# Overlapping the four token mixers of a hybrid diffusion block, with fillers that load up to four weight tiles ahead

## The chip, the cores and the metric

The kernel runs on one core of one Trainium2 chip. The metric is the device time of one execution in microseconds (us), from the core's own clock; less is better. Each kernel was timed in several executions, and one further execution was taken with the hardware profiler.

## The reference

The block has two layers. Each normalises the tokens (512 latent, 256 context, 1024 channels), projects them with one wide matrix `w_in`, runs four token mixers side by side on slices of that projection, merges them, and ends with a feed-forward part of 4096 channels:

```python
for l in range(DEPTH):                       # 2 layers
    hl = rmsnorm(x, ln1_g[l]) * (1 + sc1) + sh1          # sc, sh, g from c @ w_mod
    hc = rmsnorm(xc, ln1_g[l]) * (1 + csc1) + csh1
    zl, zc = hl @ w_in[l], hc @ w_in[l]
    ya = hyena(zl[..., :1536])               # long convolution by FFT, 2 orders
    yb = global_attention(...)               # 4 heads, 2 key heads, latent sees latent + context
    yc = mlstm(...)                          # 4 heads, both directions
    yd = window_attention(...)               # 8 heads, 2 key heads, band of 128
    acc = sum(sigmoid(gate[n]) * (y[n] @ w_up[l, n]) for n in range(4))
    x = x + g1 * (acc @ w_out[l])
    x = x + g2 * (relu(h2 @ w1 + b1) ** 2 @ w2 + b2)     # h2: normed, modulated x
return rmsnorm(x, final_g)
```

Context tokens go through the same weights, in the first layer to the end and in the second only as far as latent tokens read them.

## The kernel before, in words

All arithmetic is in 32-bit. A weight tile of 128 x 512 numbers (256 KB) is loaded by one DMA into a raw tile (four buffers), a high part is cast from it on ScalarE (ACT, L193), and the low rest is formed on GpSimd (POOL, L177); the pair sits in one of six buffers (`wp`, L112; `load`, L309). A projection (`proj`, L323) multiplies such a pair with the high and the low part of the tokens: 12 matmuls of 512 columns per half weight block, 24 where the 256 context columns come along.

The kernel is written as Python generators that a planner plays out in order of a clock of its own (`clk`). Each generator emits some instructions and yields the time after which its next step may go (the constants in `WT`, L38). The planner's order is what TensorE (PE) executes: every matmul is tied behind the one emitted before it (`in_order`, L202). The other engines' orders are made by the framework's scheduler from the same program.

There are two kinds of work. The **main line** is the mixers, one after the other: window attention (`wa`), global attention (`ga`), mLSTM (`ml`), Hyena (`hy`). `run` (L1551) plays one generator to its end. Wherever its next step isn't due, `fill_step` (L1528) plays one step of a **filler**: the queue `jobs` holds gate projections (`gt`) and the merges `mg3`, `mg1`, `mg2` of mixers that are done, `mods` holds the projection that gives the modulation (`mod`), `side` the spectrum of Hyena's filters (`spec`). Fillers must have their weights loaded ahead: `prefetch` (L1492) walks the queue and keeps at most two of each kind loaded or running, and a filler counts as ready `WT["lw"]` = 7.0 after its load was issued.

A mixer takes its own weights through `intake` (L709): it issues the two loads of its first column block, yields `LEAD` = 7.0, and then, block by block, issues the loads of the next block ahead of the projection of the present one. A flag (`busy`) lets only one intake run at a time. `wa` and `ga` go by four groups of query heads; in `wa` a group is 12 steps of scores, softmax and values (8 in the second layer), and in `ga` 6 (4). Each group but the last has in its middle the intake of the next group's query (`next_query`, `rows`). `pipe` (L1467) keeps two of a group's generators alive at once. `ml` goes by four heads, `mix(h)` beside `head(h + 1)`, whose intake takes three blocks; `hy` by four channel tiles, each two convolutions with tables that it loads at its very start (`hyena_branch`, L1303; the loads are L1318).

At the layer's level (L1955 to L1982) a loop makes one mixer's generator, runs it to its end, then appends the merge units of that mixer to `jobs`. After `wa` it first plays fillers until `side` is empty. Behind the last mixer `drain` plays what is left of the fillers, and the last merge, the output projection and the feed-forward part follow. Pools that two mixers share: 17 tiles of 768 columns (`slot`), 8 of 1024 (`big`), and in PSUM two double-bank tiles (`p2`), from which projections, scores and transposed scores all come.

Of the kernel before, what the change touches and what calls it, by code (L numbers as in the profile page):

```python
# [25 lines left out]
SEQ = 512  # L26
CTX = 256
# [4 lines left out]
HY0, GA0, ML0, WA0, GT0 = 0, 1536, 2560, 4624, 5392  # L32
LAT = (0, SEQ)
CTXS = (SEQ, CTX)
NT, NS = 17, 8
LEAD = 7.0
PACE = {"hy0": 6, "hy1": 2.55, "mlp": 7}
WT = {"wa1": 4.0, "wa2": 1.4, "waq": 6.0, "wak": 3.0, "gap": 3.19, "gaq": 2.0, "ga1": 4.0, "ga2": 1.4, "gas": 6.0,  # L38
# [4 lines left out]
class Unit:  # L43


    def __init__(self, lab, body, pre=None, kind=None, end=False, after=0.0):
        self.lab, self.body, self.pre, self.kind, self.end, self.after = lab, body, pre, kind, end, after
        self.loaded = False

# [54 lines left out]
def hybrid_block(ctx: ExitStack, tc: tile.TileContext, I, C, out, dbg=None, stop=None):  # L106
# [10 lines left out]
    cnt, ph, clk, last, busy = [0], ["pre"], [0.0], [None], [False]  # L117
# [32 lines left out]
    def acc_tile(segs, filler=False):  # L150

        if filler:
            return [(t0, n, pf1()[:, :n]) for t0, n in segs]
        w, t = span(segs), p2()
        return [(w.start, w.stop - w.start, t[:, w])]
# [189 lines left out]
    def span(segs):  # L345
        a = min(s[0] for s in segs)
        b = max(s[0] + s[1] for s in segs)
        return slice(a, b)
# [357 lines left out]
    def hview(hH, hL):  # L706
        return lambda k: (hH[:, k, :], hL[:, k, :])

    def intake(l, specs, mov, paired=None):  # L709

        def weights(col, segs, permute, use):
            w = I["w_in"][l][:, col : col + P]
            return [load((lambda raw, x=x: permute(raw, x)) if permute else wcols(w, x)) for x in range(2)]

        while busy[0]:
            yield 0.4
        busy[0] = True
        ahead = weights(*specs[0])
        if paired:
            second = weights(*specs[1])  # L720
        yield LEAD
        for i, (col, segs, permute, use) in enumerate(specs):
            W = ahead
            if paired and i < 2:
                if i == 0:
                    Ws = W, second
                    ps2 = [acc_tile(t[1]) for t in specs[:2]]
                    yield from paired(ps2, Ws, mov)
                else:
                    ahead = weights(*specs[2])  # L730
                use(ps2[i])
                continue
            if i + 1 < len(specs):
                ahead = weights(*specs[i + 1])
            ps = acc_tile(segs)
            yield from proj(ps, W, mov)
            use(ps)
        busy[0] = False
# [33 lines left out]
    def window_branch(l, vt, mov, segs, ymk, late, paired):  # L772
        w = span(segs)
# [79 lines left out]
        def next_query(j):  # L853
            yield from intake(l, [query(j)], mov)
            yield WT["waq"]
            Q[j] = stack_q(rope2(*Q[j], segs), segs)
# [56 lines left out]
        for j in range(4):  # L913
            items = [step(j, i, r) for i in range(nblk) for r in range(2)]
            if j < 3:
                items.insert(3, next_query(j + 1))
            yield from pipe(items)

    def global_branch(l, vt, mov, segs, ymk):
        w = span(segs)  # L920
# [111 lines left out]
        for h in range(4):  # L1032
            items = [step(h, i) for i in range(nblk)]
            if h < 3:
                items.insert(2, rows(1 if h == 1 else None, h + 1))
            yield from pipe(items)

    def mlstm_branch(l, vt, mov, segs, ymk):

        w = span(segs)  # L1040
# [8 lines left out]
        for x in range(2):  # L1049
            H, L = (t.rearrange("p k n -> p (k n)") for t in whalf())  # L1050
            nc.gpsimd.memset(H.bitcast(F32), 0.0)
            nc.gpsimd.memset(L.bitcast(F32), 0.0)
            quad = lambda t: t.rearrange("p (k g c) -> p k g c", k=4, g=4)
            low(quad(H)[:, :, :, 0:4], quad(L)[:, :, :, 0:4], quad(raw[:, x * 64 : x * 64 + 64]), heng=nc.vector)
            W.append([t.rearrange("p (k n) -> p k n", k=4) for t in (H, L)])
        pg = acc_tile(full)
        yield from proj(pg, W, mov)
        gb = tiny(8, "gb")
# [239 lines left out]
        yield from pipe([columns(), head(0)])  # L1298
        yield WT["mlh"]
        for h in range(4):  # L1300
            yield from pipe([mix(h)] + ([head(h + 1)] if h < 3 else []))

    def hyena_branch(l, vt, mov, segs, ymk, near_end):  # L1303
        tabs = {}
        for n in (SEQ, CTX) if CTXS in segs else (SEQ,):
            kt, nb = n // 256, n // P
            fw = [big(name="dft") for _ in range(2)] if n == SEQ else None
            t = big(name="dft") if n == CTX else None
            tv = []
            for j, nm in enumerate(("ap", "am", "tp", "tm")):  # L1310
                k = kt if j < 2 else nb
                c = n if j < 2 else n // 2
                if n == SEQ:
                    b_ = big(name="dft") if j >= 2 else fw[j]
                    v = b_.rearrange("p (k n) -> p k n", k=k)
                else:
                    v = t[:, j * 256 : (j + 1) * 256].rearrange("p (k n) -> p k n", k=k)
                nc.sync.dma_start(v, C[f"{nm}{n}"].rearrange("(k p) n -> p k n", p=P))  # L1318
                tv.append(v)
            tabs[n] = tv  # L1320
        w = span(segs)
        U = {}

# [87 lines left out]
                yield WT["hy5"]  # L1411
                U[ct].append(None)

        yield from inputs(0)
        yield WT["hy5"]
        if len(segs) > 1:
            for ct in range(4):
# [71 lines left out]
    jobs, side, mods = deque(), deque(), deque()  # L1489
    cur = [None, 0.0, None]  # L1490

    def prefetch():  # L1492

        for q, kind in ((jobs, "w"), (mods, "r")):
            n = 1 if cur[0] is not None and cur[0].kind == kind else 0
            for u in itertools.islice(q, 6):
                if u.pre is None:
                    continue
                if n >= 2 or not u.loaded and u.after > clk[0] + 1e-6:
                    break  # L1500
                if not u.loaded:
                    ph[0] = u.lab
                    u.pre()
                    u.loaded, u.after = True, clk[0] + WT["lw" if kind == "w" else "lr"]
                n += 1
# [6 lines left out]
    def next_fill():  # L1512

        if cur[0] is not None:
            return cur[1]
        return min([q[0].after for q in queues()] + [1e9])
# [11 lines left out]
    def fill_step():  # L1528
# [19 lines left out]
        ph[0] = mine  # L1548
        return True

    def run(lab, gen, pace=0):  # L1551

        ready, i = clk[0], 0
        while True:
            if ready <= clk[0] + 1e-6:
                if WT["eager"] and cur[0] is None and cur[2] is None and side and side[0].after <= clk[0]:
                    fill_step()
                ph[0] = lab
                try:
                    ready = next(gen) + clk[0]  # L1560
                except StopIteration:
                    return
                i += 1
                if pace and i % pace == 0:
                    fill_step()
            elif not fill_step():
                clk[0] = min(ready, max(next_fill(), clk[0] + 0.05))
# [37 lines left out]
    def merge_units(l, n, mov, segs, yd, gd=None, first=False):  # L1605
# [38 lines left out]
        for m in range(KD):  # L1644
            if gd is None:
                us += gate_units(l, n, m, mov, segs, tanh_to(m), after)
            us.append(Unit(f"mg{n}x{l}", body(m), pre(m), "w", end=True, after=after))
        return us

    def last_merge(l, n, gd, segs, yd, out_):  # L1650
# [262 lines left out]
    for l in range(DEPTH):  # L1913
# [38 lines left out]

        if l == 0:
            first_jobs()
        yds = {}  # L1955
        for n, lab, branch in ((3, "wa", window_branch), (1, "ga", global_branch), (2, "ml", mlstm_branch),
                               (0, "hy", hyena_branch)):
            yds[n], mk = ymaker(l, n, segs)
            res, extra = [], []
            if n == 3:  # L1960
                extra = [late, by_pieces(full, hdone) if l else by_halves]
            elif n == 0:
                merge = last_merge(l, 0, gd[0], segs, yds[0], res)
                extra = [lambda: next(merge)]
            strand = branch(l, vt, mov, segs, mk, *extra)
            if l and n == 3:
                strand = pipe(before + [then(hdone, full, first_jobs), strand], 9)
            run(f"{lab}{l}", strand, pace=PACE.get(f"{lab}{l}", 0))
            if n == 3 and l == 0:
                vturn(False)  # L1970
            if n == 2 and l == 0:
                vloads(True, nc.sync)
                vloads(False, nc.sync)
            if n == 0 and l == 0:
                vturn1(True)
                vturn1(False)
            while n == 3 and side:
                if not fill_step():
                    clk[0] = max(next_fill(), clk[0] + 0.05)
            if n:  # L1980
                jobs.extend(merge_units(l, n, mov, segs, yds[n], gd.get(n), first=n == 3))
        drain()  # L1982
        sc2 = mod_scale(l, vt, 4, "ln2_g")
        run(f"mg0x{l}", merge)
        ts(modT[l][:, 16:24, :], modT[l][:, 16:24, :], 0.5, None, ALU.mult)
        ph[0] = f"out{l}"
        if l + 1 < DEPTH:
            mods.extend(mod_units(l + 1, range(4)))
        hH = hp.tile([P, KD, TOT], F32R, tag="hH", name=uid("hH"))
# [80 lines left out]
```

## Time and profile before

| | before |
|---|---|
| median of three runs | 3309.09 us (3302.64 to 3313.1) |
| the profiled execution, its own time | 3312.71 us |
| its span, first to last instruction | 3310.9 us |
| PE busy | 3101.9 us, 94% of the span |
| weight loads into PE | 2624.0 us, 79% |
| VectorE (DVE), ACT, POOL busy | 1388.3, 1130.3, 1371.1 us |
[...]

A row of the stage view gives, for a stretch of the span, its length, each engine's busy time with the number of instructions in it, then the granted TensorE clock in parts of full speed, the busy share of the 16 DMA engines and their GB/s. A row of a timeline gives start, duration, engine, line, operation, out<-in and the count; in brackets stands how long the engine sat idle before it and what ended that.

The stages of the first layer's mixers are, by the first and last matmul of each: `wa` to 414 us, `ga` 425 to 693, `ml` 693 to 979, `hy` 983 to 1239. In the second layer they are `wa` to 2222, `ga` 2225 to 2424, `ml` 2424 to 2667, `hy` 2672 to 2843.

### The profile page before, as it was taken

To read this page: it belongs to the slowest core of one execution; us is meant where nothing else is said; L and a number is where in the kernel's file an instruction comes from. 1 tells how busy PE (TensorE), PEld (TensorE's weight loads), DVE (VectorE), ACT (ScalarE), POOL (GpSimd) and SP (SyncE) were. 2 spreads that over 40 slices of the span, in tenths; PEclk is the share of its full clock that TensorE was granted. 3 is DMA by queue.
4 is the path that set the end of the run, shared out by engine and by line. 5 is a ranking of instruction groups with operands and counts; after the bars stand their busy time and mean duration, and the time that the engine had idled before them with its cause. 6 is when DMAs were issued, how large, how long until landed. Compare 5 with 4: busy or idle time off the path is not lost. (4 is left out here: it accounts for less than half of the span.)

```text
span 3310.9 us, 48561 instructions
## 1 busy us (share of the span) xinstructions
PE 3101.9 (94%) x18320; PEld 2624.0 (79%) x18320; DVE 1388.3 (42%) x2920; ACT 1130.3 (34%) x2132; POOL 1371.1 (41%) x1126
## 2 busy tenths in 40 slices
PE   7888989899999999999999987899999999989999
PEld 5777778788888888788888876777777788778887
DVE  6644522554444454411222266434454434442223
ACT  5434423234332122322222254333343422243333
POOL 4422332324354453444433355223333455555553
PEclk9999999999999999899999988999999999989999
DMA  7343443333243455222222334444333343823332
GB/s 269 106 116 98 123 149 92 94 103 104 77 146 91 146 176 184 65 73 74 71 76 74 92 103 116 143 138 114 99 108 100 108 136 116 266 74 96 99 96 80
DMA packets 556922, 380.24 MB, mean 115 GB/s; under 512 B 45177, under 2 KB 503870, under 8 KB 556688
## 3 DMA queue, kind: packets, MB, share of 16 engines
q1 hardware_dynamic: 556056, 376.98, 37.9%
q8 instruction: 145, 2.38, 0.3%
q14 instruction: 89, 0.73, 0.1%
q10 hardware_dynamic: 632, 0.16, 0.0%
HBM read 307.52 MB, written 63.75 MB: 112 GB/s over the span
## 5 line engine op out<-in xcount | busy, mean ns | idle before, releaser
L177 POOL TENSOR_TENSOR mlp__wL<-mlp__raw,mlp__wH 128x512 fp32r<-128x512 f32 x268 | 354.6, 1324 | 469.3 <-ACT mlp__wH L193 321.8
L193 ACT CAST mlp__wH<-mlp__raw 128x512 fp32r<-128x512 f32 x268 | 166.1, 621 | 514.9 <-PE mlp__p L215 365.4
L177 POOL TENSOR_TENSOR gt__wL<-gt__raw,gt__wH 128x512 fp32r<-128x512 f32 x128 | 168.1, 1319 | 278.7 <-ACT gt__wH L193 220.2
L215 PE MATMUL mlp__p<-out__hL,mlp__wH 128*128 128x512 f32 (+1 forms) x784 | 272.3, 358 | 9.6 <-DVE out__hL L517 8.5
L215 PE MATMUL mlp__p<-out__hH,mlp__wH 128*128 128x512 f32 (+1 forms) x784 | 271.5, 358 | 1.8 <-ACT out__hH L516 1.8
L180 DVE SCALAR_TENSOR_TENSOR mlp__x<-mlp__p,modT,mlp__x 128x512 f32<-128x512 f32 (+1 forms) x169 | 106.3, 656 | 323.8 <-PE mlp__p L215 323.8
L215 PE MATMUL mlp__p<-mlp__y,mlp__wH 128*128 128x512 f32 (+1 forms) x672 | 232.0, 356 | 0.0
L215 PE MATMUL mlp__p<-mlp__aL,mlp__wH 128*128 128x512 f32 (+1 forms) x672 | 231.2, 355 | 0.0
L177 DVE TENSOR_TENSOR mlp__aL<-mlp__mq,mlp__y 128x768 fp32r<-128x768 f32 (+1 forms) x64 | 82.7, 1292 | 335.1 <-ACT mlp__y L193 335.0
L215 PE MATMUL mlp__p<-out__hH,mlp__wL 128*128 128x512 f32 (+1 forms) x784 | 181.8, 355 | 0.0
L215 PE MATMUL gt__m<-mod__hH,gt__wH 128*128 128x512 f32 (+1 forms) x512 | 172.8, 353 | 8.1 <-DVE spec__filt L177 3.2
L215 PEld LDWEIGHTS mlp__p<-out__hL,mlp__wH 128*128 128x128 f32 x784 | 151.4, 193 | 35.2 <-DVE out__hL L517 12.5
L215 PEld LDWEIGHTS mlp__p<-out__hH,mlp__wH 128*128 128x128 f32 x784 | 151.5, 193 | 23.9 <-issue 2.2
L215 PE MATMUL gt__m<-mod__hL,gt__wH 128*128 128x512 f32 (+1 forms) x512 | 167.6, 343 | 0.0
L177 POOL TENSOR_TENSOR ml__wL<-ml__raw,ml__wH 128x512 fp32r<-128x512 f32 x64 | 84.5, 1321 | 190.6 <-ACT ml__wH L193 171.0
L215 PE MATMUL mlp__p<-mlp__y,mlp__wL 128*128 128x512 f32 (+1 forms) x672 | 155.8, 354 | 0.0
L215 PEld LDWEIGHTS mlp__p<-out__hH,mlp__wL 128*128 128x128 f32 x784 | 135.3, 193 | 19.7
L215 PEld LDWEIGHTS mlp__p<-mlp__y,mlp__wH 128*128 128x128 f32 x672 | 126.8, 189 | 20.1 <-issue 2.4
L215 PEld LDWEIGHTS mlp__p<-mlp__aL,mlp__wH 128*128 128x128 f32 x672 | 127.1, 189 | 18.0
L193 ACT CAST gt__wH<-gt__raw 128x512 fp32r<-128x512 f32 x128 | 79.3, 619 | 178.2 <-DMA gt__raw<-in_w_in_dram 113.0
L215 PEld LDWEIGHTS mlp__p<-mlp__y,mlp__wL 128*128 128x128 f32 x672 | 115.0, 189 | 17.6
L215 PEld LDWEIGHTS gt__m<-mod__hH,gt__wH 128*128 128x128 f32 x512 | 98.7, 193 | 21.6 <-DVE spec__filt L177 5.2
(567 smaller groups left out, 7906.4 us busy)
## 6 DMA issues: line engine op xcount, KB each, us to landing
mlp__raw<-in_mlp_w_dram SPq DMA_DIRECT2D x240, 256.0 KB
mod__raw<-in_w_mod_dram SPq DMA_DIRECT2D x160, 256.0 KB
gt__raw<-in_w_in_dram SPq DMA_DIRECT2D x128, 256.0 KB
ml__raw<-in_w_in_dram SPq DMA_DIRECT2D x64, 256.0 KB
hy__raw<-in_w_in_dram SPq DMA_DIRECT2D x48, 256.0 KB
spec<-spec__kk SPq DMA_DIRECT2D x80, 128.0 KB
ga__raw<-in_w_in_dram SPq DMA_DIRECT2D x32, 256.0 KB
hy__spec<-spec SPq DMA_DIRECT2D x16, 512.0 KB
```

The source lines that it names most:

```text
L177: (eng or nc.vector).tensor_tensor(o, a, b, op)
L180: nc.vector.scalar_tensor_tensor(o, a, s, b, op0, op1)
L193: nc.scalar.copy(H, src)
L215: in_order(nc.tensor.matmul(ps, lhsT=a, rhs=b, start=start, stop=stop_), cost)
```

## The change

The four mixers of a layer become generators of one `pipe` of depth four under a single `run`. Each is wrapped in `staged`, which polls until a hint names it: `wa` at once, `ga` from an item put at place 3 of `wa`'s last group, `ml` from place 2 of `ga`'s last group, `hy` from beside `mix(3)` of `ml`. What stood behind a mixer in the loop (appending its merges, waiting for `side`, some small loads) now stands at its generator's end. `intake` sets the fillers' depth to two when it begins and to four when it has issued its last block's loads, and calls `prefetch` there, ahead of that block's projection. Merges with a stored gate (`mg2`) stay at two. `ml` yields `LEAD` between loading its gate weights and projecting them, and `hy` loads its tables once `ml` has ended, instead of first thing.

```diff
+    def hint(n):
+        near.add(n)
+        yield 0.0
 def intake(l, specs, mov, paired=None):
-        busy[0] = True
+        busy[0], room[0] = True, 2
...
             if i + 1 < len(specs):
                 ahead = weights(*specs[i + 1])
+            else:
+                room[0], mine = 4, ph[0]
+                prefetch()
+                ph[0] = mine
...
 # window_branch, last group          (NEAR = 3)
+            else:
+                items.insert(NEAR, hint("ga"))
 # global_branch, last group
+            else:
+                items.insert(2, hint("ml"))
 # mlstm_branch
+        yield LEAD
         pg = acc_tile(full)
...
-            yield from pipe([mix(h)] + ([head(h + 1)] if h < 3 else []))
+            yield from pipe([mix(h)] + ([head(h + 1)] if h < 3 else [hint("hy")]))
 # hyena_branch
-        for n in (SEQ, CTX) if CTXS in segs else (SEQ,):
+        def tables(n):
...
+        def late_tables():
+            while "ml" not in ended:
+                yield 0.3
+            for n in (SEQ, CTX) if CTXS in segs else (SEQ,):
+                tables(n)
-        yield from inputs(0)
+        yield from pipe([inputs(0), late_tables()])
 # prefetch
-                if n >= 2 or not u.loaded and u.after > clk[0] + 1e-6:
+                if n >= (room[0] if kind == "w" and not u.wide else 2) or not u.loaded and u.after > clk[0] + 1e-6:
                     break
+    def staged(lab, n, strand, first=None):
+        while n not in near:
+            yield 0.3
+        if first:
+            first()
+        while True:
+            ph[0] = lab
+            try:
+                lat = next(strand)
+            except StopIteration:
+                break
+            if begun_[-1:] != [lab]:
+                begun_.append(lab)
+            yield lat
 # the layer's loop
+        def mixer(n, lab, branch):
...
+            yield from staged(f"{lab}{l}", lab, strand, (lambda: vturn(False)) if n == 1 and l == 0 else None)
+            while n == 3 and side:
+                yield 0.2
...
             if n:
-                jobs.extend(merge_units(l, n, mov, segs, yds[n], gd.get(n), first=n == 3))
+                jobs.extend(merge_units(l, n, mov, segs, yd, gd.get(n), first=n == 3))
+            ended.add(lab)
+        run("", pipe([mixer(*a) for a in ((3, "wa", window_branch), (1, "ga", global_branch), (2, "ml", mlstm_branch),
+                                          (0, "hy", hyena_branch))], 4), pace=lambda: PACE.get(begun_[-1], 0))
         drain()
```

## Rows read from the trace of the kernel before

**Rows 1.** The page: span and engines' busy time.

```profile
span 3310.9 us, 48561 instructions
PE 3101.9 (94%) x18320; PEld 2624.0 (79%) x18320; DVE 1388.3 (42%) x2920; ACT 1130.3 (34%) x2132; POOL 1371.1 (41%) x1126
```

**Rows 2.** Stage view of the mixers; the last row sums nine stretches, 88:1245 and 2012:2855.

```profile
88.00:425.00 337.00, 295.02 (x2071) 245.03 (x2071) 174.26 (x497) 140.73 (x310) 104.16 (x97) 0.96 0.39 115
...
2012.00:2225.00 213.00, 186.87 (x1282) 150.43 (x1279) 100.31 (x284) 85.54 (x185) 68.34 (x56) 0.94 0.45 131
...
2424.00:2672.00 248.00, 229.93 (x1230) 189.68 (x1230) 117.07 (x245) 98.45 (x190) 104.81 (x82) 0.98 0.39 114
...
sum 2000.00, PE 1858.45 PEld 1578.43 DVE 920.36 ACT 689.67 POOL 777.41; mean PE 206.50 PEld 175.38 DVE 102.26 ACT 76.63 POOL 86.38
```

**Rows 3.** Stage view: wa to ga and its second part, ga to ml, ml to hy.

```profile
414.00:441.00 27.00, 18.95 (x125) 15.51 (x122) 4.96 (x17) 7.12 (x14) 5.44 (x6) 0.91 0.80 268
...
425.00:445.00 20.00, 14.32 (x58) 11.84 (x59) 1.94 (x6) 4.34 (x7) 7.58 (x6) 0.78 0.81 266
...
683.00:703.00 20.00, 20.00 (x133) 18.20 (x132) 5.98 (x18) 5.37 (x14) 4.88 (x4) 1.00 0.31 99
...
2662.00:2682.00 20.00, 20.00 (x92) 16.49 (x91) 6.79 (x10) 6.86 (x11) 12.01 (x10) 1.00 0.50 148
```

**Rows 4.** Timeline of PE at the first hand-over, wa to ga in layer 0.

```profile
424.35 0.64 PE L217 MATMUL mod__m<-mod__raw,scp 128*32 128x128 f32 x16 [1.88 <-ACT spec__od L677]
...
440.82 0.80 PE L215 MATMUL ga__p<-mod__hH,ga__wH 128*128 128x512 f32 x1 [5.68 <-ACT ga__wH L193]
```

**Rows 5.** Timeline of SyncE's queue (SP) at the same place.

```profile
427.20 4.29 SPq L1601 DMA_DIRECT2D mg3x__y<-yd  x7
432.68 0.38 SPq L315 DMA_DIRECT2D ga__raw<-in_w_in_dram  x1
```

**Rows 6.** Stage view of five stretches that follow an intake inside a group.

```profile
2038.00:2069.00 31.00, 23.57 (x135) 18.89 (x135) 15.38 (x31) 10.14 (x21) 14.73 (x14) 0.83 0.27 80
2098.00:2124.00 26.00, 21.43 (x136) 16.94 (x136) 11.41 (x26) 10.95 (x23) 10.16 (x7) 0.93 0.43 123
2152.00:2178.00 26.00, 21.87 (x153) 17.85 (x152) 11.75 (x29) 9.53 (x22) 6.60 (x5) 0.87 0.39 113
580.00:604.00 24.00, 17.24 (x126) 14.89 (x127) 16.12 (x36) 3.85 (x11) 7.73 (x5) 0.86 0.17 52
312.00:324.00 12.00, 7.28 (x36) 6.63 (x35) 7.55 (x15) 5.66 (x10) 4.14 (x3) 0.72 0.34 96
```

**Rows 7.** Timeline of PE inside the first of these.

```profile
2053.81 1.07 PE L215 MATMUL gt__m<-mlp__hH,gt__wL 128*128 128x512 f32 x4
2054.72 0.71 PE L227 MATMUL wa__p<-ident,wa__wp 128*128 128x128 f32 x5
2062.24 1.30 PE L227 MATMUL wa__p<-ident,wa__wp 128*128 128x128 f32 x5 [6.81 <-DVE wa__p L868]
```

**Rows 8.** Timeline of ACT in the same stretch.

```profile
2056.43 0.62 ACT L193 CAST gt__wH<-gt__raw 128x512 fp32r<-128x512 f32 x1 [3.62 <-DMA gt__raw<-in_w_in_dram]
2056.96 1.25 ACT L805 CAST wa__wqX<-wa__wr 64x512 fp32r<-64x512 f32 x2
```

**Rows 9.** Timeline of PE: the end of ml in layer 1.

```profile
2641.70 0.49 PE L215 MATMUL ml__p<-ml__mV,ml__mW 128*128 128x129 f32 x2 [1.48 <-ACT ml__ST L1209]
...
2647.57 0.82 PE L215 MATMUL ml__p<-ml__mV,ml__kw 128*128 128x129 f32 x4 [2.47 <-DVE ml__kw L172]
```

**Rows 10.** Groups on PE from 2843.4 to 2854.6, the end of hy in layer 1.

```profile
L215 PE MATMUL mg2x__m<-mg2x__y,mg2x__wH 128*128 128x512 f32 x32 | 8.1, 395 | 0.0
L215 PE MATMUL mg2x__m<-mg2x__y,mg2x__wL 128*128 128x512 f32 x16 | 4.3, 389 | 0.0
```

**Rows 11.** SP's timeline: the last of the eight loads of Hyena's tables, layer 0.

```profile
961.21 0.56 SPq L1318 DMA_DIRECT2D hy__dft<-const_tm_dram  x1
```

**Rows 12.** Instructions that read those tables; the first start stands ahead of "to".

```profile
L215 PE MATMUL hy__p<-hy__fF,hy__dft x576: 270/275/422, 1020.1 to 2837.4; 128*128 128x128 f32 x192
```

More of the change, by code (lines that the diff above doesn't have):

```diff
@@ L34 @@
 CTXS = (SEQ, CTX)
-NT, NS = 17, 8
+NT, NS, NEAR = 17, 8, 3
 LEAD = 7.0
@@ L47, in __init__ @@
         self.lab, self.body, self.pre, self.kind, self.end, self.after = lab, body, pre, kind, end, after
-        self.loaded = False
+        self.loaded, self.wide = False, False
 VROWS = [
@@ L1490, in hybrid_block @@
     cur = [None, 0.0, None]
+    room = [2]
     def prefetch():
@@ L1549, in fill_step @@
         return True
+    def staged(lab, n, strand, first=None):
[12 more added lines that the diff above has]
+            yield lat
+    near, ended, begun_ = set(), set(), [""]
     def run(lab, gen, pace=0):
@@ L1563, in run @@
                 i += 1
-                if pace and i % pace == 0:
+                every = pace() if callable(pace) else pace
+                if every and i % every == 0:
                     fill_step()
@@ L1647, in merge_units @@
             us.append(Unit(f"mg{n}x{l}", body(m), pre(m), "w", end=True, after=after))
+            us[-1].wide = gd is not None
         return us
@@ L1954, in hybrid_block @@
             first_jobs()
[L1955 to L1959, printed above, removed]
+        near.clear()
+        ended.clear()
+        near.add("wa")
+        merges, strands = [], []
+        def mixer(n, lab, branch):
+            yd, mk = ymaker(l, n, segs)
+            extra = []
             if n == 3:
@@ L1962, in hybrid_block @@
             elif n == 0:
-                merge = last_merge(l, 0, gd[0], segs, yds[0], res)
-                extra = [lambda: next(merge)]
+                merges.append(last_merge(l, 0, gd[0], segs, yd, res))
+                extra = [lambda: next(merges[0])]
             strand = branch(l, vt, mov, segs, mk, *extra)
@@ L1967, in hybrid_block @@
                 strand = pipe(before + [then(hdone, full, first_jobs), strand], 9)
-            run(f"{lab}{l}", strand, pace=PACE.get(f"{lab}{l}", 0))
-            if n == 3 and l == 0:
-                vturn(False)
+            yield from staged(f"{lab}{l}", lab, strand, (lambda: vturn(False)) if n == 1 and l == 0 else None)
+            while n == 3 and side:
+                yield 0.2
             if n == 2 and l == 0:
@@ L1976, in hybrid_block @@
                 vturn1(False)
-            while n == 3 and side:
-                if not fill_step():
-                    clk[0] = max(next_fill(), clk[0] + 0.05)
             if n:
-                jobs.extend(merge_units(l, n, mov, segs, yds[n], gd.get(n), first=n == 3))
+                jobs.extend(merge_units(l, n, mov, segs, yd, gd.get(n), first=n == 3))
+            ended.add(lab)
+        res = []
+        run("", pipe([mixer(*a) for a in ((3, "wa", window_branch), (1, "ga", global_branch), (2, "ml", mlstm_branch),
+                                          (0, "hy", hyena_branch))], 4), pace=lambda: PACE.get(begun_[-1], 0))
+        merge = merges[0]
         drain()
@@ L1985, in hybrid_block @@
         ts(modT[l][:, 16:24, :], modT[l][:, 16:24, :], 0.5, None, ALU.mult)
-        ph[0] = f"out{l}"
+        ph[0], room[0] = f"out{l}", 2
         if l + 1 < DEPTH:
```

## The prediction

> **What bounds the kernel now.** I read the page's busy times first [rows 1]: PE works 3101.9 of 3310.9 us, so it is the bound, and 209 us of the span is all that PE idles. No other engine is above half. The change adds and removes no matmul, no load and no cast; it only reorders. So it can win idle time of PE and time at the lower of its two clock levels, and nothing else, and it can lose the same.
>
> Then I asked where that time lies. The stages that the change touches are nine stretches of 2000 us together, in which PE is busy for 1858.45, so idle for 141.55 us [rows 2]. The stretches of the window mixer carry the most: 42.0 us idle of 337 in layer 0 and 26.1 of 213 in layer 1, at granted clocks of 0.96 and 0.94. [...]
>
> The hand-overs came third, since the change is about them. They are nearly seamless already: PE is busy 20.00 of 20 us from `ga` to `ml` in layer 0 and from `ml` to `hy` in layer 1 [rows 3]. Fillers cover them. One is not: `wa` to `ga` in layer 0 has 8.05 us idle in 27, and the 20 us from 425 on run at 0.78 [rows 3]. Two waits make it, 1.88 us and 5.68 us; the second is `ga`'s projection waiting for its own weights [rows 4]. The reason stands in SP's queue: seven loads of `mg3`'s inputs were issued from 427.20 on, and `ga`'s next weights behind them at 432.68 [rows 5].
>
> Last, the large idle stretches inside mixers. Five follow an intake that ran inside a group, and hold 119 − 91.39 = 27.6 us idle, summed over the five rows [rows 6]. In the first, the last gate unit ends at 2054.88, the transposes follow, and then PE sits for 6.81 us with no filler put in, until DVE's softmax comes through [rows 7]. ACT shows why DVE is late: a cast of a filler's weights waited 3.62 us for its load, and the two casts that finish the rotated query stood behind it [rows 8].
>
> **The change, part by part.** The sums are against the profiled execution's own 3312.7 us, which lies 3.6 us above the median of 3309.1.
>
> A. `wa` to `ga`, layer 0. `ga`'s six weight loads are issued while `wa`'s last group runs, and `mg3`'s inputs are asked for only when `wa` has ended, so the order of [rows 5] turns round. Removed: the 5.68 us, plus the slow clock, 0.22 x 20 = 4.4 us [rows 3]; the 1.88 us wait for the filter's spectrum finds `ga`'s projections to cover it. I take −11; the ends are 0 and −12.4 (8.05 idle and 4.4 clock). The other five hand-overs give nothing, as they have nothing: the 20 us of projection that now slide under the preceding mixer only push fillers to a later place.
>
> B. Four tiles ahead. Two at most gives two units per load latency, after which PE has none. With four loaded when an intake takes its last block, one or two more units of 2.9 us stand ready in each of the five stretches. Their idle 27.6 us, and the clock, 0.17 x 31 + 0.07 x 26 + 0.13 x 26 + 0.14 x 24 + 0.28 x 12 = 17.2 us [rows 6], make 45 at most. The planner puts a filler in only where its own clock says that the mixer waits; in [rows 7] it had put the mixer's transposes there, believing them due. So most of such a wait stays. I take a third, −14, and for the ends 0 and −40. The casts of the two further tiles lie beside PE on ACT and POOL, which are 34% and 41% busy [rows 1].
>
> C. `hy`'s first projections under `ml`'s last head. In layer 1 that head has waits of 1.48 and 2.47 us with no filler in them [rows 9]. I take −4; 0 to −10, the latter if half of all idle time there, 248 − 229.93 = 18.1 us [rows 2], goes too.
>
> D. New waits where two mixers overlap. `wa` and `ga` steps take their score tiles from the same two PSUM tiles as a projection. The nearest rows are the intakes inside groups, of which there are three per layer in `wa` and in `ga`, twelve in all: five cost (27.6 + 17.2) / 5 = 9 us each [rows 6], the others little, so 3.7 on average. The change makes four new such places (`wa` to `ga`, `ga` to `ml`, two layers). With fillers deeper than before I take 2.5 each, +10; the ends are 0 (a gain there is already counted in A) and +36.
>
> E. Fillers used sooner are missing later. At the end of layer 1's `hy`, four `mg2` units run alone for 11.2 us [rows 10]; layer 1 can win that much before `hy`'s last convolution stands bare, and B to D give it some 6. I take +2 for layer 0; up to +10.
>
> F. Hyena's tables are now asked for after `ml`. In layer 0 the last was issued at 961.21, 22 us ahead of `hy`'s first projection and 59 ahead of the first transform on them at 1020.1 [rows 11, 12]. What sets the issue is when `ml`'s large tiles come free, and this stays; 0. If it were issued only at `ml`'s end, the first transform, which the planner then places some 7.6 later by its constants, would wait: 2 MB at the 266 GB/s that a loaded stretch shows [rows 3] is 7.9 us plus the issue, so up to +5 per layer.
>
> SP's queue: the extra two loads per intake go in front of the query's small rotation loads, but ahead of a projection of 24 matmuls; no DMA is added. The new `LEAD` in `ml` costs nothing as `ga`'s last steps and fillers run under it; without them it is up to 7. The pacing of fillers now counts the polls too; ±3.
>
> Sum: −11 − 14 − 4 + 10 + 2 = −17, so 3295.7 for that execution and **3292** against the median. A difference of 0.3%, 10 us, is about what a measurement of this kernel can tell from none.
>
> **Rivals.**
>
> 1. *All starvation goes and nothing new comes.* Ends of A, B and C, −62: 3247. For it: in all five stretches PE stood without a filler. Against it: [rows 7, 8] show a chain through ACT and DVE that fillers on PE don't shorten.
>
> 2. *Only the order changes.* Five of six hand-overs have no idle time [rows 3], and gains and new waits cancel: 3309, within 10 either way. That the change does less than it says comes to the same: an intake waits until the preceding mixer's is done, so the overlap may be short.
>
> 3. *Slower: a filler's cast ahead of the mixer's work on ACT.* The row shows one cast that waited 3.62 us for its load with the query's casts behind it [rows 8] and PE idle for 6.81 us [rows 7]. With four loads going out together beside the mixers', such a cast can stand ahead of each of the six query intakes in `wa` and the four overlaps. One more 3.62 us at ten places, and half as much again for the clock, is +54; with A to C that is 3312.7 − 29 + 54 = 3338, or 3334 against the median. It decides from 2.9 us per place on (29 / 10). For it: [rows 8]. Against it: the number of casts is the same, and a tile loaded two units sooner has more time to land. [...]
>
> **How the numbers follow.** Forecast (10 to 45 us gained) 0.40; rival 1, 0.16; rival 2, 0.20; rival 3, 0.24. So faster 0.56, same 0.20, slower 0.24. The range 3254 to 3328 holds the forecast, rival 2, and the nearer half of rivals 1 and 3, which is 0.8; as both signs are in it, the forecast's own range is 3264 to 3299.
>
> **What would show it.** A: no wait of `ga` on its weights, and the clock near 1.00 around the new hand-over in layer 0. B: gate units in the places of [rows 6], and less than 20 us idle in layer 1's window stage. C: `hy` projections between `ml` steps of the last head. D: waits on DVE or ACT by `ga` or `ml` projections, or by `wa` and `ga` score matmuls, in the last groups. E: fewer than four `mg2` units alone at the end of layer 1's `hy`, and idle time in its last convolution. F: no wait for `dft`. Wrong would be a PE idle sum in these stages that isn't smaller by some 15 us, or waits behind filler casts on ACT at most query intakes (rival 3).

## The result, and the profile after

The changed kernel takes **3362.3 us** (median of 4) where the kernel before, run beside it, takes 3308.2 (median of 4): a ratio of **1.0157**, 95% interval 1.0144 to 1.0171. It is slower by 1.6%, outside the range that was given. (Ratios here and below are those on record; the two medians alone give 1.0163, and a difference of 0.1% is noise.)

The page's busy times after, in the form of [rows 1]:

```profile
span 3355.1 us, 48561 instructions
PE 3119.3 (93%) x18320; PEld 2640.9 (79%) x18320; DVE 1409.0 (42%) x2920; ACT 1126.4 (34%) x2132; POOL 1374.2 (41%) x1126
```

The count of matmuls is unchanged. The span of the profiled execution grew by 44.2 us (the medians differ by 54): PE idles 235.8 us instead of 209.0 (26.8 more), and the same 18320 matmuls take 17.4 us more, at a mean granted clock of 0.964 where it was 0.969.

The stage view of the mixers after, with the columns of [rows 2] (length, busy time of PE, PEld, DVE, ACT and POOL, granted clock, DMA share, GB/s). The first four are `wa`, `ga`, `ml` and `hy` of layer 0; then come `wa`, the overlap, `ga`, `ml` and `hy` of layer 1, each moved with the work:

```profile
88.00:446.00 358.00, 303.40 (x2036) 251.22 (x2038) 170.09 (x473) 138.57 (x301) 109.43 (x99) 0.94 0.35 102
446.00:690.00 244.00, 227.15 (x1559) 199.94 (x1555) 109.61 (x267) 75.82 (x161) 73.62 (x58) 0.96 0.35 107
690.00:1013.00 323.00, 310.04 (x1904) 265.86 (x1903) 152.45 (x328) 121.22 (x241) 118.61 (x83) 1.00 0.36 109
1013.00:1274.00 261.00, 247.81 (x1497) 219.76 (x1496) 122.01 (x244) 56.00 (x104) 132.62 (x118) 0.96 0.47 150
2041.00:2254.00 213.00, 184.27 (x1230) 148.00 (x1228) 95.00 (x270) 82.90 (x178) 69.98 (x58) 0.94 0.48 137
2254.00:2303.00 49.00, 42.16 (x271) 35.35 (x272) 17.08 (x39) 11.07 (x23) 15.71 (x12) 0.93 0.27 78
2303.00:2492.00 189.00, 166.91 (x1053) 141.42 (x1052) 73.03 (x165) 56.58 (x113) 56.97 (x47) 0.94 0.38 110
2492.00:2757.00 265.00, 256.24 (x1360) 212.62 (x1359) 134.17 (x250) 108.51 (x205) 128.09 (x97) 0.99 0.42 120
2757.00:2903.00 146.00, 137.37 (x731) 119.30 (x732) 66.30 (x130) 33.56 (x55) 81.62 (x78) 0.95 0.53 161
sum 2048.00, PE 1875.35 PEld 1593.47 DVE 939.75 ACT 684.23 POOL 786.64; mean PE 208.37 PEld 177.05 DVE 104.42 ACT 76.03 POOL 87.40
```

All of the loss is here: 2048 us for what took 2000 [rows 2], with 172.65 us idle instead of 141.55. It comes in both layers, most of it in `wa` and `ga`, and `hy` idles more too (8.6 us of 146 in layer 1); `ml` in layer 1 got better (8.8 us idle, 18.1 before).

Where PE waits is seen by asking for the fillers alone. The stage view of three stretches of the changed kernel, all instructions:

```profile
470.00:518.00 48.00, 37.54 (x257) 32.66 (x256) 25.72 (x69) 18.95 (x39) 19.26 (x16) 0.89 0.54 168
2220.00:2296.00 76.00, 58.43 (x415) 47.84 (x413) 26.80 (x79) 23.61 (x51) 18.20 (x15) 0.87 0.35 101
2453.00:2531.00 78.00, 60.35 (x399) 52.94 (x398) 43.38 (x83) 25.70 (x46) 19.79 (x15) 0.87 0.41 119
```

and the same stretches, only what touches the gate units' accumulator (length, PE, PEld, ACT, then as above):

```profile
470.00:518.00 48.00, 2.74 (x19) 2.43 (x18) 0.98 (x2) 0.89 0.54 168
2220.00:2296.00 76.00, 0.30 (x2) 0.00 (x0) 0.60 (x1) 0.87 0.35 101
2453.00:2531.00 78.00, 0.00 (x0) 0.00 (x0) 0.00 (x0) 0.87 0.41 119
```

In 202 us the gate units take 3.0 us of PE and the merges as good as nothing (`mod` and `spec` take some 15), PE idles 45.7 us, at a clock of 0.87 to 0.89. The gate units are used up, and the next ones are queued with a merge, when a mixer has ended (in layer 0, after `side` is empty too). So my first theory after the result was that fillers run out (T2), beside casts in front of the mixers' work on ACT (T1, rival 3) and waits where mixers overlap (T3).

T1 could be seen as well. ACT, DVE and PE at one place of layer 0's `wa`, three timelines of the changed kernel (start, duration, engine, line, operation, count, idle time before and what ended it):

```profile
179.40 0.62 ACT L193 CAST gt__wH<-gt__raw 128x512 fp32r<-128x512 f32 x1 [4.47 <-DMA gt__raw<-in_w_in_dram]
...
181.31 0.24 ACT L193 CAST wa__yH<-wa__p 128x128 fp32r<-128x128 f32 x1
```

```profile
181.59 0.29 DVE L177 TENSOR_TENSOR wa__yL<-wa__p,wa__yH 128x128 fp32r<-128x128 f32 x1 [7.41 <-ACT wa__yH L193]
```

```profile
182.33 0.39 PE L215 MATMUL wa__p<-wa__wkH,wa__wqX 128*128 128x256 f32 x1 [3.48 <-DVE wa__p L877]
```

A filler's cast waits 4.47 us for its load, the mixer's cast stands behind it and a second one, DVE waits for that, and PE loses 3.48 us: the chain of [rows 7, 8] once more. Whether such places make the loss, a trace cannot say; runs can.

### The profile page after: what moved, and what is told of

It reads as the page before. It is cut to its first block, busy times and chain, and to the rows that moved or that the text cites. A ratio compares the mean times of both kernels' runs of the same rounds, so it can differ in the third digit from the quotient of the medians.

```text
span 3355.1 us, 48561 instructions
## 1 busy us (share of the span) xinstructions
PE 3119.3 (93%) x18320; PEld 2640.9 (79%) x18320; DVE 1409.0 (42%) x2920; ACT 1126.4 (34%) x2132; POOL 1374.2 (41%) x1126
```

## The experiments

Differences between runs are differences of ratios times 3309 us; a ratio's interval is some ±0.2%, 5 to 7 us, and that of a difference of two some 7 to 11. "Above the control" is against the run with both parts taken out. A wait is bare when no filler covers it.

**The two parts, one by one.** Two ahead: `room[0], mine = 4, ph[0]` becomes `2`. No overlap: the next mixer's hint is given where the preceding one ends:

```diff
-                items.insert(NEAR, hint("ga"))
+                items.insert(NEAR, hint("x"))
...
             ended.add(lab)
+            near.add({"wa": "ga", "ga": "ml", "ml": "hy"}.get(lab, "x"))
```

> The change with two tiles ahead everywhere; the overlaps stay. Three theories of the 52 us that the change loses (ratio 1.0157). T1, four tiles ahead does it: their casts stand ahead of the mixers' work on ACT and DVE. Already in layer 0's window mixer, before anything overlaps, the changed kernel is 19.7 us behind at the same window matmul, with two more gate units done (about 9 us), so about 11 us lost there; with as much in layer 1 and in the other mixers, this run gives back 30 or more: ratio 1.000 to 1.006. T2, fillers that are used too soon are missing when the next ones cannot yet be queued: both parts use them sooner, so half comes back, 1.007 to 1.010. T3, the waits where two mixers overlap do it: nothing comes back, 1.013 to 1.017. I expect T1 and T2 together, 1.006.

Measured: 1.019 (1.0173 to 1.0208). A miss: no part of the loss comes back; the overlaps alone lose at least as much as the change.

> The change with each mixer begun only when the preceding one has ended, four tiles ahead kept. T1: most of the loss stays, ratio 1.010 to 1.016. T2: about half, 1.006 to 1.010, with PE idle before the next mixer's gates come. T3: none of it, 0.997 to 1.002. I expect 1.008; and in layer 0's window mixer the same 11 us lost as in the changed kernel, since its order there is the same up to the overlap.

Measured: 1.0174 (1.0154 to 1.0193). A miss: four ahead alone loses as much as both together.

> Both parts taken out: no overlap, two tiles ahead. What is left of the change is one outer loop with polling, the later Hyena tables, the pacing that counts the polls and the added lead in the mLSTM branch. PE's order is that of the kernel before up to the end of layer 0's window mixer. All three theories: 0.998 to 1.002. If it is above 1.003, a part that I had priced at nothing (tables, pacing, lead) costs, and its stage will show it.

Measured: **0.993** (0.9913 to 0.9946), 23 us faster than before. So what I had priced at nothing gains, and each named part alone costs about what both together do: 81 us (four ahead), 86 (overlaps), 75 (both), above this control. They don't add up.

> The change with two tiles ahead, and without the overlap of wa with ga alone; the overlaps of ga with ml and of ml with hy stay. Beside the run with two tiles ahead and all three overlaps it prices the overlap of wa with ga. T1: like that run, within 0.002. T3: the overlap of wa with ga is the dear one (in the changed kernel PE has no filler from 402 to 449 and waits of 2.99 and 1.74 us there), so 0.004 to 0.008 lower. T2: 0.002 to 0.005 lower. I expect 1.002.

Measured: 1.0031 (1.0021 to 1.0041). The overlap of `wa` with `ga` costs 53 us, twice what any of the theories gave it, the other two 33.

**Casts off ACT.** `load(wcols(src, x), nc.gpsimd)` for gate units; PE's order stays.

> No overlap, two tiles ahead, and the high-half cast of each gate unit's weights moved from ACT to POOL; PE's order is unchanged. It is the control for the run with four tiles ahead and the same move. POOL gets about 192 casts more and ACT as many fewer; POOL is 41% busy. Expected 0.990 to 1.003 of the kernel before (the run with both parts taken out stands at 0.993): the casts leave the queue on which softmax and evictions stand, but the low half on POOL, which needs the high half, comes a copy later.

> No overlap, four tiles ahead, the gate units' high-half casts on POOL; PE's order is that of the run with four tiles ahead alone, which stands at 1.0174, 80 us above its control. T1, the fillers' casts stand in front of the mixers' work on ACT: with ACT free of them this comes to within 25 us of the run with two tiles ahead and the same move. T2, the order is at fault, since fillers used early are missing later (in the run with four ahead alone, ga in layer 1 runs from 2456 to 2504 without one): 50 us or more remain between the two. I expect a gap of 40 us, both.

Measured: 0.9914 (0.9893 to 0.9935) and 1.0108 (1.0082 to 1.0135). (128 casts moved, not 192.) The gap is 64 us where it was 81: casts in front of ACT's queue are some 17 us of the cost of four ahead (give or take 14, by the four intervals), the order the rest.

> No overlap, three tiles ahead in place of four. There are six pairs of split weight tiles for fillers and mixers together; a mixer's intake wants two to four of them. T1 by the tiles: with three, a mixer's load finds a tile more often, so well over half of the 80 us goes: 0.996 to 1.003. T2: the order moves as much as with four, so 1.005 to 1.017. I expect 1.004.

Measured: 1.0185 (1.016 to 1.0209). A miss: three tiles lose as much as four. The cost isn't in proportion to what is held in advance.

**Gates of all mixers queued first**, so that the queue is never empty at a hand-over:

```diff
-        gd = {n: dram([KD, P, TOT], f"gate{l}_{n}") for n in (2, 0)}
+        gd = {n: dram([KD, P, TOT], f"gate{l}_{n}") for n in (2, 0, 3, 1)}
...
-            for n in (2, 0):
+            for n in (2, 0, 3, 1):
```

> The whole change, with the gates of all four mixers queued at the start of a layer (those of wa and ga too, which until now are queued with their merges, when the mixer has ended). The gate work is the same; it needs no mixer's output, so there are fillers to be had where the queue was empty: in the changed kernel PE is idle 83 us and loses 39 more to the clock in stretches of 12 us or more without a filler, 43 and 14 in the kernel before. T2, the fillers run out: 40 us or more of the loss go, ratio below 1.004. T1, casts on ACT stand in front: those stay, 1.012 to 1.018. T3, waits where mixers overlap: 1.010 or more. I expect 1.000.

> Control for the gates queued first: no overlap, two tiles ahead (this stands at 0.993 without the gates first), gates of all four first. It has fewer empty stretches to lose (45 and 13 us as in the kernel before), of which some are the waits for the merges at wa's and ga's ends, 9 us idle and 3 of clock at wa's end in layer 0; 32 gates more go through memory. T2: 0.985 to 0.993. T1: 0.993. I expect 0.989.

> Four tiles ahead without overlap, all gates first; without the gates first it stands at 1.0174, 80 us above its control. T2: the empty stretches go (93 us idle and 43 of clock in them, against 45 and 13), and what is left above the control is the cost of the casts on ACT, some 17 us by the pair of runs with those casts on POOL: 0.990 to 1.000. T1: 1.012 or more. I expect 0.995.

Measured: 1.0215 (1.0194 to 1.0236), 0.9976 (0.9964 to 0.9988), 1.0187 (1.016 to 1.0214). All three miss the time that I expected: T2 in this form falls. (The first lies where T3 had put it and the third where T1 had; the next run decides on T1.) With four ahead, more fillers to be had early are spent early, and the bare stretch turns up later. It lies in layer 1's `ml` and the start of `hy`, where no gate unit runs for 162 us (stage view, all instructions):

```profile
2614.00:2776.00 162.00, 135.53 (x660) 111.03 (x659) 58.45 (x152) 57.67 (x114) 57.79 (x47) 0.89 0.36 109
```

**Four loaded, but spent as with two.** Each unit gets a due time by the rule of two tiles, and may not start sooner; loads and casts go out four deep:

```diff
+        n = 1 if cur[0] is not None and cur[0].kind == "w" else 0
+        for u in itertools.islice(jobs, 6):
+            if u.pre is None:
+                continue
+            if n >= 2 or u.due is None and not u.loaded and u.after > clk[0] + 1e-6:
+                break
+            if u.due is None:
+                u.due = clk[0] + WT["lw"]
+            n += 1
...
-            if u.after > t or u.pre and not u.loaded:
+            if u.after > t or u.pre and not u.loaded or u.kind == "w" and u.pre and (u.due is None or u.due > t):
```

> Four tiles ahead without overlap, but a filler may be put on PE only when two tiles ahead would have let it: PE's order is matmul for matmul that of the run with both parts taken out (0.993), and only loads and casts go out sooner. T2 as it stands after the gates-first runs (a layer has a fixed stock of fillers; what is spent sooner covers little idle time and is missing later, wherever the queue is empty): the order is the cost, so 0.993 to 1.000, the excess being the casts on ACT (17 us by the pair on POOL). T1, casts and tiles held in advance are the cost: 1.010 to 1.018. I expect 0.997.

Measured: **0.9925** (0.9908 to 0.9941), the control's time. In the trace all 18320 matmuls, by their tiles, stand in the control's order, and the loads do go out sooner: from the issue of a gate tile's load to its first matmul it is 42 us in the median, 26 in the control and 36 with four ahead alone. Four tiles loaded ahead cost nothing when PE's order is that of two. T1 falls as the cause, and the order is shown to be it.

What the order does is seen first in layer 0's `wa`. In this run, all instructions and the gate units alone:

```profile
88.00:415.00 327.00, 286.87 (x2014) 238.17 (x2014) 172.12 (x491) 137.99 (x303) 106.18 (x98) 0.96 0.38 112
...
88.00:415.00 327.00, 146.73 (x744) 119.94 (x744) 14.69 (x30) 0.96 0.38 112
```

and with four ahead alone (the run of 1.0174):

```profile
88.00:438.00 350.00, 299.35 (x2048) 247.44 (x2046) 174.16 (x490) 138.34 (x303) 102.37 (x94) 0.93 0.35 103
...
88.00:438.00 350.00, 158.32 (x768) 129.30 (x768) 15.64 (x32) 0.93 0.35 103
```

There 24 more matmuls of gate units are played (some 5 us, as an estimate from 146.73 / 744; the rest of the 11.6 us goes with the clock, 0.93 for 0.96), and PE is not less idle for them but 10.5 us more (50.65 against 40.13): units that come sooner lie where they cover less. With the casts on POOL, `wa` in layer 0 is longer by as much (25 us from two ahead to four), so it isn't the casts. Next, the end of `ga` in layer 1, its last 59 us in the rationed run: all instructions, then the gate units and `mg3`'s merges alone (their columns: length, PE, PEld, ACT or DVE):

```profile
2345.00:2404.00 59.00, 54.14 (x386) 45.02 (x385) 27.75 (x65) 22.14 (x45) 18.19 (x16) 1.00 0.40 112
...
2345.00:2404.00 59.00, 14.76 (x60) 10.93 (x61) 1.19 (x2) 1.00 0.40 112
...
2345.00:2404.00 59.00, 7.06 (x30) 4.97 (x28) 2.03 (x3) 1.00 0.40 112
```

and the last 59 us of `ga` in layer 1 with four ahead alone, all instructions and gate units:

```profile
2437.00:2496.00 59.00, 42.11 (x233) 37.53 (x231) 24.46 (x60) 14.92 (x31) 13.25 (x13) 0.77 0.28 80
...
2437.00:2496.00 59.00, 0.00 (x0) 0.00 (x0) 0.00 (x0) 0.77 0.28 80
```

With gate units and merges in between, PE idles 4.9 us at full clock; without, 16.9 us at 0.77.

> The rationed run with four loaded (0.9925), the ration stretched from 7 to 9 us for two tiles. If spending sooner is what costs, spending a little later should cost little or nothing as long as the stock is used up by the layer's end: 0.990 to 0.997, with fewer gate units used in the window mixer and more merges alone at the end of each layer. If the 7 us ration is just the point that the planner's other constants were set for, and any shift costs, 1.003 or more. I expect 0.996.

Measured (`u.due = clk[0] + 9.0`): 1.0184 (1.0162 to 1.0206). A miss, on the expectation's other branch, and it corrects the theory: spending *later* costs 86 us, as much as spending sooner. Now waits stand bare in layer 0's `wa` already (53.7 us idle, 40.1 in the rationed run), and what isn't spent there is left over: after Hyena's last matmul there follow 119 matmuls of gate units and merges other than Hyena's own in layer 0 and 143 in layer 1, where the rationed run has 0 and 35. `wa` of this run and a stretch in it, all instructions, then the gate units in that stretch:

```profile
88.00:421.00 333.00, 279.33 (x1918) 230.67 (x1916) 170.87 (x487) 136.96 (x298) 102.45 (x94) 0.93 0.36 104
...
321.00:340.00 19.00, 11.57 (x81) 8.87 (x80) 14.61 (x38) 9.38 (x19) 6.95 (x6) 0.82 0.38 106
...
321.00:340.00 19.00, 0.19 (x2) 0.00 (x0) 0.39 (x1) 0.82 0.38 106
```

**The single overlaps.**

> Two tiles ahead, and of the three overlaps that of ml with hy alone. With both late overlaps the run stands at 1.0031, 32 us above the run with none. If hy's projections only move under ml's last head (my step C), 0.991 to 0.995; if they take the place of the fillers that ml's waits want, and hy's end stands bare for it, 0.998 to 1.003. In the run with both, hy in layer 1 has 10.7 us idle and 8.5 of clock against 2.9 and 0, so I expect 0.999.

Measured: 0.9971 (0.9959 to 0.9983), between the two ranges: 14 us above the control for `ml` with `hy`, so 20 for `ga` with `ml`. What `hy` costs more stands in its own stage of layer 1, first in the control, then here:

```profile
2649.00:2828.00 179.00, 176.06 (x920) 150.33 (x919) 78.00 (x143) 48.43 (x79) 104.92 (x96) 1.00 0.50 153
```

```profile
2678.00:2854.00 176.00, 167.36 (x872) 142.10 (x871) 72.61 (x137) 44.20 (x73) 98.42 (x91) 0.99 0.51 155
```

2.9 us idle become 8.6, with its projections already done under `ml`.

> Two tiles ahead, all three overlaps, but ga begins when 8 in place of 3 steps of wa's last group of 12 (8 in layer 1) have been taken up, so the overlap of wa and ga is shorter. With 3 it is 1.019, without that overlap 1.0031. T3, two mixers in each other's way for as long as they overlap: in between, 1.004 to 1.012. T2, the loss comes from the merges queued later and from wa's end: nearly as with 3, 1.013 to 1.019. I expect 1.010.

Measured (`items.insert(8, hint("ga"))`): 1.0114 (1.0099 to 1.0129), between 1.0031 without this overlap and 1.019 with the long one. Its length counts, as T3 had it and T2 had not. What the length does is seen at the layer's end. The stage from Hyena's last matmul to the feed-forward part in layer 0, first in the control, then with all three overlaps, and of the latter 55 us of `mg2`'s merges alone, of which 12.2 idle at a clock of 0.84:

```profile
1231.00:1265.00 34.00, 33.86 (x194) 29.63 (x193) 24.46 (x28) 10.55 (x15) 10.44 (x7) 1.00 0.76 253
```

```profile
1198.00:1313.00 115.00, 101.16 (x529) 85.40 (x528) 34.57 (x46) 21.30 (x34) 46.60 (x31) 0.93 0.74 245
...
1224.00:1279.00 55.00, 42.80 (x195) 34.23 (x196) 8.39 (x16) 4.96 (x8) 23.63 (x17) 0.84 0.85 281
```

With the overlaps the mixers of layer 0 end 33 us sooner, but fewer fillers have been played beside them. Matmuls of gate units and merges other than Hyena's own that follow Hyena's last one, in layers 0 and 1: 0 and 35 in the control, 71 and 83 for `ml` with `hy` (14 us above it), 119 and 107 for the two late overlaps (33), 263 and 107 with the shorter first one (61), 335 and 143 with all three (86). So the overlaps spend fillers later, and four ahead, which leaves 0 and 0, spends them sooner.

**The small parts**, each undone in the control: the lead in `ml`, the late tables, the pacing.

> The run with both parts taken out (0.993, 21 us faster than before), and the lead of 7 us ahead of the mLSTM's gate projection taken out too. PE's order is then that of the kernel before up to Hyena in layer 0. If the lead was the gain (fillers stand where the projection waited for its weights), this is 0.998 to 1.001; if the tables or the pacing were, it stays at 0.991 to 0.995. I expect 0.997.

> Both parts taken out, and Hyena's tables asked for at its start, as before the change, instead of after ml's end. It tells which of the small parts gave the 21 us that the run without both parts gains on the kernel before: the lead did not (0.9938 without it). If the late tables did, 0.998 to 1.001; if the pacing that counts the polls did, 0.992 to 0.995. I expect the latter, as Hyena's stage in layer 0 is the one that got shorter and the pacing sets its fillers.

> Both parts taken out, and Hyena's pacing counted by its own steps, as before the change. The run with both parts out gains 21 us on the kernel before; the lead (0.9938 without) and the later tables (0.9945 with the early ones) each leave that gain. If the pacing is it: 0.997 to 1.001. If each is a part of it or one stands for the other: 0.992 to 0.996. I expect 0.998.

Measured: 0.9938 (0.9919 to 0.9958), 0.9945 (0.9927 to 0.9964), 0.9942 (0.9927 to 0.9957). None of the three alone is the gain of 23 us. Half of it lies in Hyena's stage of layer 0, 256 us from first to last matmul before, 240 to 245 in the control and these three; which combination gives it, or what else the single loop reorders, stays open.

**A version that beats both.** The rationed run with the casts on POOL:

> The rationed run with four loaded, and the gate units' high-half casts on POOL. The two runs that each beat the kernel before stand at 0.9925 (rationed) and 0.9914 (two ahead, casts on POOL). If the casts on ACT still delay the mixers there, 0.986 to 0.991; if the ration has already taken that away, 0.991 to 0.994. I expect 0.990.

Measured: 0.9918 (0.9901 to 0.9935). It, the rationed run, the one with two ahead and casts on POOL, and the control itself can't be told apart; each is some 0.8% faster than the kernel before and some 2.4% faster than the change. With the right order, casts on ACT cost nothing that can be measured.

## Why the prediction was wrong

**The step that failed is E, with B on which it rests; for the overlaps it is the zero in A.** Either part of the change alone makes the whole loss. B took the units that stand ready as free: they would go into the five starved stretches and take a third of their idle time, −14. E then priced their absence elsewhere at +2, up to +10, at the end of `hy`. Measured, four ahead alone costs +81. (E's signs came, no `mg2` unit left behind `hy` in layer 1 and 8.6 us idle in it; the place and the price were wrong.) Units that are ready sooner are put on PE at the planner's first waits, where they cover little (the rows of layer 0's `wa` above), and are missing at later ones; the absence shows at the ends of `wa` and `ga` (the stretches above), not at the layer's alone, and beside 45.8 us more of idle time than in the control the same matmuls take 42.7 us more, at a mean clock of 0.961 for 0.977 (the pages in the last section). The limit of two tiles, which I read as a shortage, was the ration that spread a fixed stock of fillers over the mixers' waits.

*A.* The hand-over's wait for weights is gone; what is left in 402:446 is this (stage view after):

```profile
402.00:446.00 44.00, 37.34 (x215) 30.14 (x217) 10.97 (x38) 10.71 (x27) 6.36 (x5) 0.89 0.11 31
```

6.7 us idle at 0.89, against 8.05 and 0.91 in [rows 3]: the −11 was not had, and by the pair of runs this overlap costs 53. "Only push fillers to a later place" was said of the other five hand-overs and called nothing; the count of fillers left at the layer's end grows with the cost of the overlaps, as listed above, and there PE idles 12.2 of 55 us at a clock of 0.84 with all three.

*B's sign to look for*, under 20 us idle in layer 1's window stage, is wrong: 28.7 us, 26.1 before [rows 2].

*C.* Right in its place: `ml`'s idle time in layer 1 went from 18.1 to 8.8 us, near the −10 end. But the overlap as a whole costs 14; in layer 1, 5.7 us of it is idle time in `hy`.

*D.* As new waits by two mixers in each other's way it stays small where I looked (the longest at the first overlap of the changed kernel is 2.99 us, on ACT). As the price of two overlaps, +10 with an upper end of +36, it is 53 and 20; how much of that is such waits no run tells apart from the fillers' places.

*F, lead and pacing.* F at 0 holds (0.9945 early, 0.993 late). The three small parts together, priced at 0 ± 3, are worth −23.

*Rival 3* had the right side and half the size (3334, so +25), but not the cause. Its chain is there (the three timelines above): the mixer's cast starts at 181.31, behind a filler's that waited 4.47 us for its load. That ACT is held up so at ten places, as priced, was not shown. And moving those casts off ACT gives back 17 of 81 us, and with PE's order kept, the same early casts on ACT cost nothing (0.9925). Its point of decision, 2.9 us per place, was priced as if the place were always on the path.

What stays argued, not shown: why so many shifts of the fillers (sooner, later, `ga` overlapped with `wa`) land some 60 to 90 us above their controls, and why two of them together cost no more than one. My reading is that the planner's constants fit one order, in which the fillers lie on the real waits, that a shift loses most of that cover, and that it can be lost only once. The 9 us ration speaks for it, as it changes one constant only. Against its general form stand the gates first with two ahead, another order from the end of layer 0's `wa` on, at 15 us, and the overlaps of 14 and 20.

## What to carry to other kernels

In an order that a planner fixes, a limit on prefetch may be the rate at which filler work is spent; before raising it, ask what the fillers cover later, and count them as a stock. To test a prefetch depth, keep the compute order and change the loads alone, as the rationed run does: the two effects were 0 and 81 us. Take a compound change apart before you judge it, since here only the parts that were priced at nothing gained.

## What the runs showed of the hardware

Between these two runs the span grows by nearly twice what PE's idle time does. Page of the control, then of four ahead alone:

```profile
PE 3080.4 (94%) x18320; PEld 2609.0 (80%) x18320; DVE 1398.1 (43%) x2920; ACT 1128.9 (34%) x2132; POOL 1370.7 (42%) x1126
```

```profile
PE 3123.1 (93%) x18320; PEld 2646.5 (79%) x18320; DVE 1403.0 (42%) x2920; ACT 1129.6 (34%) x2132; POOL 1371.7 (41%) x1126
```

With spans of 3278.2 and 3366.7 us, PE idles 197.8 and 243.6: 45.8 us more idle, and the same 18320 matmuls take 42.7 us more, at a mean granted clock of 0.961 against 0.977. For the change it is 26.8 and 17.4. (The control's profiled execution was its quickest, 9 us under its median.) Of the first 3300 stretches of 1 us, the granted clock is 1.00 in 3072 and 0.50 in 165 before the change, and in 3021 and 200 after it; in the 63 and 79 others it lies between.

A one-input cast of 128x512 took POOL 660 ns where it took ACT 619; POOL's two-input subtraction took 1335, twice its cast. The groups on POOL in the run with two ahead and casts on POOL, then on ACT and DVE there at the same size (busy us, mean ns, then idle before):

```profile
L177 POOL TENSOR_TENSOR gt__wL<-gt__raw,gt__wH 128x512 fp32r<-128x512 f32 x128 | 169.7, 1335 | 6.8 <-PE ml__p L215 2.7 <-PE hy__p L215 0.6
...
L191 POOL CAST gt__wH<-gt__raw 128x512 fp32r<-128x512 f32 x128 | 84.3, 660 | 243.7 <-DMA gt__raw<-in_w_in_dram 167.9 <-PE spec__m L215 19.9 <-PE gt__m L215 18.3
```

```profile
L193 ACT CAST wa__wH<-wa__raw 128x512 fp32r<-128x512 f32 x32 | 19.4, 619 | 48.1 <-DMA wa__raw<-in_mlp_w_dram 35.1 <-DMA wa__raw<-in_w_in_dram 7.8 <-PE wa__p L215 3.8
...
L177 DVE TENSOR_TENSOR mlp__aL<-mlp__mq,mlp__y 128x512 fp32r<-128x512 f32 x32 | 48.6, 1518 | 119.4 <-ACT mlp__y L193 119.4
...
L177 DVE TENSOR_TENSOR mg0x__mL<-mg0x__ac,mg0x__y 128x512 fp32r<-128x512 f32 x8 | 5.8, 723 | 1.1 <-ACT mg0x__y L193 1.1
...
L191 DVE CAST ga__gqH<-ga__gr 128x512 fp32r<-128x512 f32 x4 | 1.7, 413 | 0.0
```

Two-input operations took DVE 1518 ns in one group and 723 in another, beside POOL's 1335; the one-input cast took DVE 413 beside POOL's 660.
